# Row sums of 16384 x 1024: which rows a partition owns

## The chip, the cores and the metric

One core of one Trainium2 chip runs the kernel. The metric is device time in microseconds (us), the median of several runs. A profiled execution gives the durations of single instructions and of single DMA packets; its span runs from the first to the last instruction, and is a little shorter than the device time of the same execution.

## The reference

```python
def setup_inputs():
    batch, seq, dim = 32, 512, 1024
    return {
        "x": np.random.randn(batch, seq, dim).astype(np.float32),
        "multiplier": 0.5,
    }

def reference(x, multiplier):
    return (np.sum(x, axis=-1) * multiplier).astype(np.float32)
```

The 16384 rows of x hold 1024 floats (4 KiB) each, 67.1 MB in all; the result is one float per row, 64 KiB.

## The kernel before

The core has 128 partitions, so each of them sums 128 rows. The rows are split in three parts, in the order in which they lie in memory.

- The blocks: `own` = 112 rows for each partition, in seven blocks of 16 rows. Partition p owns the 112 rows from 112p, so a block is 16 neighbouring rows, 64 KiB in one run, for each partition.
- The tail: 15 rows for each partition (`x_last`), the 15 rows from 128 x 112 + 15p. They come in five pieces: p0 (7 rows), p1 (5), p2 (2), and the last row cut at column 608 into two pieces of its own, e0 and e1, in the tensor `end`.
- The lead: the last 128 rows of x, one for each partition (`x_lead`). It is loaded first of all, and its sums are turned by a transpose so that they are stored as four runs of 32.

All transfers are issued by SP on one queue, in this order: lead, blocks 0 to 6, p0, p1, p2, e0, e1 (line 83 in the helper `load`), the store of the blocks' results (line 167), the lead's store (171), the tail's store (195). Three buffers of 16 rows hold the blocks in turn; block b from 3 on waits until DVE has reduced block b - 3 (`freed`), and the tail's pieces wait in the same way (line 156). The lead and blocks 0 to 2 wait for nothing; `start_loads_at_entry` (line 203) moves their issues ahead of the barrier that the engines pass at the start.

DVE reduces a block in one instruction (line 134) and scales its sums (line 140). Of block 6 DVE takes eight rows, and ACT the other eight, row by row, with an activation that accumulates (`act_row`, line 90). In the tail `on_act` lists ACT's rows; DVE adds the others with `dve_sum`, which adds the two halves of a row and accumulates (line 100). The two pieces of the last row are summed one after the other, the second together with the first one's sum. The tail's store waits for both engines, and SP then waits for all three stores.

Twice the access pattern of a transfer matters. One is the source of a block, `x_rows[:, c0 : c0 + B, :]`: 128 runs of 64 KiB, 448 KiB apart. The other is the source of a tail's piece: 128 runs, 60 KiB apart.

Of the kernel before, what the change touches and what calls it, by code (L numbers as in the profile page):

```python
# [9 lines left out]
def kernel(  # L10
# [18 lines left out]
    P = nc.NUM_PARTITIONS  # L29
# [3 lines left out]
    x_flat = x.flatten_outer_dims()  # L33
    N, D = x_flat.shape
    rows = N // P
    out_flat = out.rearrange("b s -> (b s)")
    mul = float(multiplier)

    B = 16
    n_blocks = rows // B  # L40
    assert N == P * rows and rows == n_blocks * B
    own = rows - B
    tail = B - 1
    lead0 = P * (own + tail)
    x_rows = x_flat[0 : P * own, :].rearrange("(p c) d -> p c d", p=P)
    x_last = x_flat[P * own : lead0, :].rearrange("(p c) d -> p c d", p=P)
    x_lead = x_flat[lead0:N, :]
    out_rows = out_flat[0 : P * own].rearrange("(p c) -> p c", p=P)
    out_last = out_flat[P * own : lead0].rearrange("(p c) -> p c", p=P)
    out_lead = out_flat[lead0:N].rearrange("(q c) -> q c", c=32)  # L50

# [22 lines left out]
    def marks(i, engine):  # L74

        s = dve_done if engine == "dve" else act_done
        i.then_inc(s, 1)
        counts[engine] += 1
        return counts[engine]

    def load(name, dst, src, free=None):
        landed = sem(name)
        i = nc.sync.dma_start(out=dst, in_=src)  # L83
        if free is not None:
            i.wait_op(dve_done, free, "sem-ge")
        i.then_inc(landed, 16)
        return landed

    def act_row(t, r, col):
        return nc.scalar.activation(  # L90
            out=t[:, r, :],
            in_=t[:, r, :],
            func=mybir.ActivationFunctionType.Copy,
            scale=mul,
            accum_out=res[:, col : col + 1],
        )

    def dve_sum(row, dst, scale):
        mid = row.shape[-1] // 2
        return nc.vector.tensor_tensor_reduce(  # L100
            out=row[:, 0:mid],
            in0=row[:, 0:mid],
            in1=row[:, mid:],
            scale=scale,
            scalar=0.0,
            op0=ADD,
            op1=ADD,
            accum_out=dst,
        )
# [3 lines left out]
    freed = []  # L113
    lead_landed = load("lead_landed", lead, x_lead)
    for b in range(n_blocks - 1):
        c0 = b * B
        t = buf[b % bufs]
        landed = load(
            f"landed{b}",
            t,  # L120
            x_rows[:, c0 : c0 + B, :],
            freed[b - bufs] if b >= bufs else None,
        )
        h = B if b < n_blocks - 2 else B // 2
        if b == 0:
            nc.vector.wait_ge(lead_landed, 16)
            nc.vector.wait_ge(dve_done, zeroed)
            summed = marks(dve_sum(lead, lead_sq[:, 0:1], mul), "dve")
            turned = nc.vector.transpose(out=lead_tr, in_=lead_sq)  # L129
            turned.wait_op(dve_done, summed, "sem-ge")  # L130
            marks(turned, "dve")
        nc.vector.wait_ge(landed, 16)
        done = marks(
            nc.vector.reduce_sum(  # L134
                out=sums[:, c0 : c0 + h], in_=t[:, 0:h, :], axis=mybir.AxisListType.X
            ),
            "dve",
        )
        freed.append(done)
        scaled = nc.vector.tensor_single_scalar(  # L140
            out=res[:, c0 : c0 + h],
            in_=sums[:, c0 : c0 + h],
            scalar=mul,
            op=mybir.AluOpType.mult,
        )
        scaled.wait_op(dve_done, done, "sem-ge")
        early_dve = marks(scaled, "dve")
        if h < B:
            nc.scalar.wait_ge(landed, 16)
            for r in range(h, B):  # L150
                i = act_row(t, r, c0 + r)
            early_act = marks(i, "act")

    c0 = (n_blocks - 1) * B
    t = buf[(n_blocks - 1) % bufs]
    nc.sync.wait_ge(dve_done, freed[n_blocks - 1 - bufs])
    pieces = [(0, 7), (7, 12), (12, 14)]
    landed = [
        load(f"landed_p{k}", t[:, lo:hi, :], x_last[:, lo:hi, :])
        for k, (lo, hi) in enumerate(pieces)  # L160
# [11 lines left out]
    lead_stored = sem("lead_stored")  # L172
    lead_store.then_inc(lead_stored, 16)

    on_act = {4, 5, 6, 10, 11, 13}
    for k, (lo, hi) in enumerate(pieces):
        on = [r for r in range(lo, hi) if r in on_act]
        nc.scalar.wait_ge(landed[k], 16)
# [86 lines left out]
```

## Time and profile before

| What | us |
| --- | --- |
| Median of 3 runs (lowest, highest) | 160.66 (160.62, 160.67) |
| The profiled execution | 160.62 |
| its span | 159.28 |
| DVE busy (39 instructions) | 120.2 |
| ACT busy (29 instructions) | 16.3 |
| A block's reduction on DVE, 16 rows | 17.22 |
| DVE's idle time ahead of its seven reductions, all waiting for x | 30.3 |
| First reduction of a block starts | 22.81 |
| Second and third start | 42.25, 61.61 |
| Block 6: DVE and ACT start on it | 139.02 |
| The tail's store is issued | 157.80 |

DMA moved 67.18 MB in 2168 packets, 422 GB/s over the span. A reader of such a profile should ask first which resource has no gaps, and then what the start and the end add to it. "DVE" is the vector engine, "ACT" the scalar engine, "SP" the engine that issues the transfers here, "SPq" its queue of issues. A line of a timeline gives start, length, engine, source line, operation, output, input, count, and in brackets how long the engine was idle before and what ended that.

### The profile page before, as it was taken

The numbers are of one execution on the slowest core, as the hardware profiler recorded it, in microseconds if no ns is written. First come the engines' busy times: TensorE is split into PE (matmuls) and PEld (weight loads), VectorE is DVE, ScalarE is ACT, GpSimd is POOL, SyncE is SP. The second block draws the span as 40 slices with busy tenths as digits, with TensorE's granted clock in tenths as the row PEclk, the third lists the DMA queues.
The fourth block names the chain that finished last, engine by engine and source line by source line (L and its number), as shares of the span: only waits on it lengthen the run. The fifth ranks groups of instructions, "written<-read, shape, count | busy, mean of one in ns | idle before, by whom it ended". The sixth has DMA issues, their size and how long they took to land.

```text
span 159.3 us, 128 instructions
## 1 busy us (share of the span) xinstructions
DVE 120.2 (75%) x39; ACT 16.3 (10%) x29; POOL 0.2 (0%) x4
## 2 busy tenths in 40 slices
DVE  2000029999499995999869997899959999599744
ACT  2000000000000000000000000000000000099844
POOL 0000000000000000000000000000000000000000
DMA  9969989899699699699699898996996996999994
GB/s 395 510 280 527 411 379 527 379 411 527 263 527 527 263 527 527 263 527 494 296 527 428 362 527 379 411 527 280 510 527 263 527 527 263 436 403 433 442 397 144
DMA packets 2168, 67.18 MB, mean 422 GB/s; under 512 B 504, under 2 KB 632, under 8 KB 888
## 3 DMA queue, kind: packets, MB, share of 16 engines
q1 hardware_dynamic: 2168, 67.18, 98.0%
HBM read 67.11 MB, written 0.07 MB: 422 GB/s over the span
## 4 chain that ended last, share of the span: by engine, by line
DMA 75%; DVE 22%; SPq 1%; issue 0%
DMA xb<-in_x_dram 52%; DMA end<-in_x_dram 24%; DVE sums L134 22%; SPq L83 1%; DVE end L100 1%; DVE res L140 0%; DVE res L100 0%
## 5 line engine op out<-in xcount | busy, mean ns | idle before, releaser
L134 DVE TENSOR_REDUCE sums<-xb 128x16 f32<-128x16384 f32 (+1 forms) x7 | 112.0, 16001 | 30.3 <-DMA xb<-in_x_dram 30.3
L90 ACT ACTIVATE xb<-xb 128x1024 f32<-128x1024 f32 x14 | 14.6, 1046 | 138.1 <-DMA xb<-in_x_dram 138.0
L100 DVE CUSTOM_DVE_ANT_0 xb<-xb 128x512 f32<-128x512 f32 x8 | 5.1, 689 | 3.9 <-DMA xb<-in_x_dram 3.9
L90 ACT ACTIVATION_READ_ACCUMULATOR xb<-xb 128x1 f32 x14 | 2.6, 188 | 0.0
L111 DVE MEMSET end<- 128x2 f32 x1 | 0.1, 60 | 2.9 <-PEq L26 2.9
L90 ACT ACT_TABLE_LOAD x1 | 1.3, 1283 | 2.9 <-PEq L26 2.9
L140 DVE TENSOR_SCALAR res<-sums 128x16 f32<-128x16 f32 (+1 forms) x7 | 1.2, 174 | 0.2
L100 DVE CUSTOM_DVE_ANT_0 end<-end 128x304 f32<-128x304 f32 (+1 forms) x2 | 0.9, 428 | 0.1
L100 DVE CUSTOM_DVE_ANT_0 lead<-lead 128x512 f32<-128x512 f32 x1 | 0.7, 693 | 0.2 <-DMA lead<-in_x_dram 0.2
L100 DVE DVE_READ_ACCUMULATOR2_ANT res<- 128x1 f32 x9 | 0.8, 83 | 0.0
L129 DVE STREAM_TRANSPOSE lead_tr<-lead_sq 128x32 f32<-128x32 f32 x1 | 0.2, 211 | 0.0
L246 POOL MEMSET const-bfloat16-1.0<- 128x1 bf16 x1 | 0.1, 101 | 0.0
L246 POOL MEMSET const-uint8-127<- 128x1 uint8 x1 | 0.1, 101 | 0.0
L246 POOL MEMSET const-float32-0.0<- 128x1 f32 x1 | 0.1, 98 | 0.2 <-issue 0.2
L246 POOL MEMSET const-float32-1.0<- 128x1 f32 x1 | 0.1, 98 | 0.0
L112 DVE MEMSET lead_sq<- 128x32 f32 x1 | 0.1, 85 | 0.0
L100 DVE DVE_READ_ACCUMULATOR2_ANT end<- 128x1 f32 x1 | 0.1, 84 | 0.0
L100 DVE DVE_READ_ACCUMULATOR2_ANT lead_sq<- 128x1 f32 x1 | 0.1, 83 | 0.0
## 6 DMA issues: line engine op xcount, KB each, us to landing
xb<-in_x_dram SPq DMA_DIRECT2D x1, 3584.0 KB, 29.9
xb<-in_x_dram SPq DMA_DIRECT2D x1, 2560.0 KB, 35.7
xb<-in_x_dram SPq DMA_DIRECT2D x1, 1024.0 KB, 37.7
lead<-in_x_dram SPq DMA_DIRECT2D x1, 512.0 KB, 3.2
end<-in_x_dram SPq DMA_DIRECT2D x1, 304.0 KB, 37.9
end<-in_x_dram SPq DMA_DIRECT2D x1, 208.0 KB, 38.0
xb<-in_x_dram SPq DMA_DIRECT2D x7, 40.8
out_dram<-res SPq DMA_DIRECT2D x1, 56.0 KB, 9.6
```

Source lines behind the costliest of these rows:

```text
L83: i = nc.sync.dma_start(out=dst, in_=src)
L90: return nc.scalar.activation(out=t[:, r, :], in_=t[:, r, :], func=mybir.ActivationFunctionType.Copy, scale=mul, accum_out=res[:, col : co ...
L100: return nc.vector.tensor_tensor_reduce(out=row[:, 0:mid], in0=row[:, 0:mid], in1=row[:, mid:], scale=scale, scalar=0.0, op0=ADD, op1=ADD, ...
L111: marks(nc.vector.memset(end[:, at - 2 : at], 0.0), "dve")
L112: zeroed = marks(nc.vector.memset(lead_sq, 0.0), "dve")
L129: turned = nc.vector.transpose(out=lead_tr, in_=lead_sq)
L134: nc.vector.reduce_sum(out=sums[:, c0 : c0 + h], in_=t[:, 0:h, :], axis=mybir.AxisListType.X),
L140: scaled = nc.vector.tensor_single_scalar(out=res[:, c0 : c0 + h], in_=sums[:, c0 : c0 + h], scalar=mul, op=mybir.AluOpType.mult,)
L246: nc = _bacc.Bacc("TRN2", target_bir_lowering=False, num_devices=1)
```

## The change

The blocks get 111 rows for each partition instead of 112, and the tail 16 instead of 15; the lead stays. Block 0 is the one that gets shorter: 15 rows, and block b from 1 on covers the rows from 16b - 1. Partition 4g + b, with b from 0 to 3 and g from 0 to 31, owns the 111 rows from 111(32b + g): neighbouring partitions with the same g now read rows 3552 apart, and with the same b and neighbouring g rows 111 apart. The store of the blocks' results follows the same pattern. In the tail partition p owns 16 rows from 128 x 111 + 16p; the pieces are 8, 5 and 2 rows and the cut last row, and `on_act` has seven rows instead of six.

```diff
-    own = rows - B
-    tail = B - 1
+    own = rows - B - 1
+    tail = B
     lead0 = P * (own + tail)
-    x_rows = x_flat[0 : P * own, :].rearrange("(p c) d -> p c d", p=P)
+    x_rows = x_flat[0 : P * own, :].rearrange("(b g c) d -> g b c d", b=4, c=own)
     x_last = x_flat[P * own : lead0, :].rearrange("(p c) d -> p c d", p=P)
     x_lead = x_flat[lead0:N, :]
-    out_rows = out_flat[0 : P * own].rearrange("(p c) -> p c", p=P)
+    out_rows = out_flat[0 : P * own].rearrange("(b g c) -> g b c", b=4, c=own)
...
     for b in range(n_blocks - 1):
-        c0 = b * B
+        c0 = max(b * B - 1, 0)
+        n = (b + 1) * B - 1 - c0
         t = buf[b % bufs]
         landed = load(
             f"landed{b}",
-            t,
-            x_rows[:, c0 : c0 + B, :],
+            t[:, 0:n, :],
+            x_rows[:, :, c0 : c0 + n, :],
             freed[b - bufs] if b >= bufs else None,
         )
-        h = B if b < n_blocks - 2 else B // 2
+        h = n if b < n_blocks - 2 else n // 2
...
-        if h < B:
+        if h < n:
             nc.scalar.wait_ge(landed, 16)
-            for r in range(h, B):
+            for r in range(h, n):
                 i = act_row(t, r, c0 + r)
             early_act = marks(i, "act")
 
-    c0 = (n_blocks - 1) * B
+    c0 = own
...
-    pieces = [(0, 7), (7, 12), (12, 14)]
+    pieces = [(0, 8), (8, 13), (13, 15)]
...
-    on_act = {4, 5, 6, 10, 11, 13}
+    on_act = {4, 5, 6, 7, 11, 12, 14}
```

## The prediction

> **What bounds the kernel now.** I read the chain of waits first, then the busy slices, the groups by shape, the transfers' issues, the timeline of the end, and last the trace's records of single DMA packets (start, duration and size of each).
>
> The chain, in order of time (start, length, what):
>
> ```profile
> 0.90 41.33 DMA xb<-in_x_dram
> ...
> 42.25 17.23 DVE sums L134
> ...
> 59.50 40.80 DMA xb<-in_x_dram
> ...
> 100.32 17.23 DVE sums L134
> ...
> 118.91 37.93 DMA end<-in_x_dram
> ...
> 156.87 0.50 DVE end L100 x2
> 157.37 0.02 issue
> 157.39 0.38 DVE end L100
> ```
>
> The two reductions stand in it only because they free the buffer of a load that is issued long before its bytes can move. What never rests is the load:
>
> ```profile
> DMA  9969989899699699699699898996996996999994
> q1 hardware_dynamic: 2168, 67.18, 98.0%
> L134 DVE TENSOR_REDUCE sums<-xb 128x16 f32<-128x16384 f32 x6 | 103.3, 17220 | 28.3 <-DMA xb<-in_x_dram 28.3
> ```
>
> The queue's packets fill 98.0% of 16 engines' time. DVE needs 17.22 us for a block that takes 19.36 us to arrive (its reductions start at 80.97 and 100.32, 19.35 apart), so it waits 1.9 us for each. The packet records say the same: each of the seven blocks is 128 packets of 64 KiB, one per partition, 8 per engine; the median packet takes 2.418 us, and 8 x 2.418 = 19.34. In the middle of the run there is nothing left to win.
>
> What is above that floor: from the first packet (1.03 us) to the end of the last (156.92) are 155.90 us. Packets at their medians would take 8 x 0.159 (lead) + 56 x 2.418 (blocks) + 8 x (1.062 + 0.761 + 0.311 + 0.098 + 0.069) (the five pieces of the tail) = 155.09. So about 0.81 us is all that a better order of reading could give. It sits mostly at the start: the 128 packets of block 0 average 2.448 instead of 2.418, 0.24 us for an engine's eight, and the worst, the first on their engines, take 2.76 and 2.81. The other six blocks are over the median by 0.12 us together. The lead's packets are over theirs by 0.22, and the lead is not changed.
>
> **The change, part by part.** The sum is made against the profiled execution: 160.62 us, of which 159.28 is the span and 1.34 lies around it; the median of the runs is 160.66.
>
> *Rows from block 0 to the tail.* Block 0 gets 15 rows, p0 8 instead of 7, so all landings from block 0 to block 6 come earlier by one row, 19.36/16 = 1.21 us, and the tail is one row longer: the last byte comes when it did. Packet counts stay. DVE: block 0 costs 15 x 17.22/16 = 16.14, saving 1.08 in a stretch where it waits for the next block anyway. In the tail DVE keeps eight rows and ACT goes from six to seven, one more step of 1.04. ACT's four rows of p0 start at its landing, about 147.5 as now, and end near 147.5 + 4 x 1.04 + 0.19 = 151.9; p1 is started at 153.63, so 1.8 us of waiting covers it. p1 and p2 keep their split (three and two, one and one), and so does the end after them:
>
> ```profile
> 156.12 0.69 DVE L100 CUSTOM_DVE_ANT_0 xb<-xb 128x512 f32<-128x512 f32 x1 [0.57 <-DMA xb<-in_x_dram]
> ...
> 156.87 0.48 DVE L100 CUSTOM_DVE_ANT_0 end<-end 128x304 f32<-128x304 f32 x1
> ...
> 157.80 0.35 SPq L195 DMA_DIRECT2D out_dram<-res  x1
> ```
>
> Sum: 0. Without that cover the ACT step would cost 1.04.
>
> *A pattern of one more level in seven loads and the early store.* The same 128 runs, but the source now steps over 32 g and 4 b. No row of the trace has such a load. The nearest issues from both sides:
>
> ```profile
> 0.43 1.38 SPq L83 DMA_DIRECT2D xb<-in_x_dram  x3
> ...
> 148.00 0.35 SPq L167 DMA_DIRECT2D out_dram<-res  x1
> 148.39 0.62 SPq L171 DMA_DIRECT2D out_dram<-lead_tr  x1
> ```
>
> A plain 128-partition load holds SP for 1.38/3 = 0.46; the one issue that is not a plain 128-partition pattern holds it for 0.62, against 0.35 for its neighbour. So 0 to 0.27 us for each; I take 0.2. For block 0 it is covered: the lead's first packet starts 1.03 us after its issue, so block 0, issued at 0.43, could start at 1.46, with the longer issue at about 1.7; it starts at 2.45, when engines have done their lead rows. Cover 0.8 us; gone, the whole 0.2 would show. Behind it on SP are blocks 1 and 2 (needed at 22 and 41 us) and SP's arrival at the start barrier: DVE's and ACT's first work (2.94, 2.87) would come up to 0.6 later, and the first block lands past 20. Later loads wait for a free buffer and still run a block ahead: the tail's five issues start at 117.6, its data moves from 138.1. Sum: 0, bound +0.27.
>
> Should such a load use fewer of the 16 engines, nothing would hide it. The Trainium skill (DMA: Bandwidth & Descriptors, "Why a DMA increments its semaphore by 16 and not by 1") says that the number of engines is the largest up to 16 that divides the slowest dimension of both sides; that is 16 for 32 and 128, so by it nothing is lost.
>
> *The addresses.* In the blocks, neighbouring partitions read 448 KiB apart now. After, partitions with the same b and neighbouring g read 444 KiB apart, those with neighbouring b 14.2 MiB. Four partitions away, the reads are 1792 KiB apart now (7 x 256 KiB, so all are at the same place within 256 KiB), and 444 KiB after (111 x 4 KiB, so all at different places). In the tail it is the reverse: pitch 60 KiB becomes 64 KiB, four partitions 240 becomes 256 KiB. No row shows the price, so bounds: at best the blocks lose their excess, 0.24 + 0.12 = 0.36 (and 0.81 if everything above the floor went); at worst the tail gains what block 0 shows now, 0.24 at the entry of each of p0, p1 and p2, +0.72. For the blocks I take the nearest rows, the tail's packets, whose spacing now is not a multiple of 256 KiB: over their medians by 0.01 (p0) and 0.02 us (p1) for an engine's eight, against 0.24. So -0.35. For the tail I take 0, since blocks 1 to 6 are aligned now and pay only 0.02 each once the engines run out of step.
>
> [...]
>
> *Stores.* The early store (444 instead of 448 B each) moves behind the loads in the queue as now (issued at 148.00, landed 9.6 us later), and the last store carries 64 instead of 60 B. Its 128 packets take 0.010 us each, 8 per engine: 0.
>
> Sum: 160.66 - 0.35 = **160.31**.
>
> **Rivals.**
>
> *The start is not a matter of addresses (no change).* The lead's packets, which read one contiguous piece, are also over their median, by 0.22 us: then the first packets are slow whatever they read, and all else is hidden. Against it: the lead is the very first reading, block 0 is not. 160.65, 160.4 to 160.9. [...]
>
> *The tail's 64 KiB pitch (slower).* The place is p2 and the two pieces of the last row, where a packet is 8 KiB, 2432 and 1664 B and every reader is at the same place within 64 KiB. Price: from +0.24 (one more entry like block 0's) to a doubling of 8 x (0.311 + 0.098 + 0.069) = +3.8; I take +0.6, 161.3. Nothing behind the last landing can absorb it: the final sums follow it within 0.02 us. It decides as soon as these three together exceed 3.82 us by more than the 0.35 won. Against: 448 KiB pitch now costs nothing in steady running.
>
> *The jumps (much slower).* An engine that goes from one b to the next leaps 14.2 MiB. If each leap cost what the first packets of block 0 cost, 0.14 us on average over the sixteen, 56 packets would give +7.9, about 168. Against: such slow packets now occur at the start only.
>
> *The change does not alter who reads when.* If the records show block 0's packets as long as before, it did nothing to the start: this is the no-change case.
>
> The Trainium skill (DMA: Bandwidth & Descriptors, "The descriptor swizzle") gives four neighbouring partitions to one engine, so that at a time the engines would be at one b and different g; no record here names the engine.
>
> **How the numbers follow.** A difference under 0.2% (0.32 us) cannot be told from none here: faster is below 160.34, slower above 160.98. Chances: the forecast 0.44, with its own range 159.95 to 160.45; no change 0.31; the tail 0.17; the jumps 0.08. The forecast's case stays within 0.2% in about a tenth of its cases, the no-change case crosses to the fast side in as many. Faster 0.43, same 0.32, slower 0.25. The range starts at 159.9 (0.81 won, less a little) and goes to 161.4, past the tail's price; outside are the jumps, and dear tails: about 0.15.
>
> **What would show it.** Right: block 0's packets (60 KiB, 2.418 x 15/16 = 2.27 us expected) without outliers of 2.5 and more; blocks still 19.35 apart; the last landing near 156.5 instead of 156.92, and the same 0.9 us from there to the last store's issue. Wrong: outliers at block 0 as before; packets of p2 or of the last row above 0.311, 0.098 and 0.069; an issue of block 0 so long that its first packet comes after 2.45 with the engines idle; blocks more than 19.4 apart; ACT still in p0 when p1 lands.

## The result, and the profile after

The changed kernel takes 162.80 us (median of 6 runs, 162.28 to 163.47) against 160.66: a ratio of 1.0136, 95% interval 1.0124 to 1.0148, so 2.1 us slower where 0.35 us faster was forecast, and outside the range. Its profiled execution took 163.47 us with a span of 162.14. Medians here and below are over all executions; the ratios leave out six that lie over 1.5% above the fastest of their kernel (two each of e2 and e16, one each of e4 and e15), and are if anything too low there.

The page of the changed kernel: the busy tenths of the DMA engines and what they moved in 40 slices, and the queue's share.

```profile
DMA  7999998997997998998998997998998999999991
GB/s 281 318 455 440 470 446 388 453 501 340 453 501 340 469 485 356 453 485 356 453 485 356 453 501 340 453 501 372 437 485 388 437 469 396 396 412 435 395 372 51
q1 hardware_dynamic: 2168, 67.18, 96.7%
```

The same 2168 packets and 67.18 MB, with a lower share of a longer span (98.0% before). The kernel before moved, in its 40 slices:

```profile
GB/s 395 510 280 527 411 379 527 379 411 527 263 527 527 263 527 527 263 527 494 296 527 428 362 527 379 411 527 280 510 527 263 527 527 263 436 403 433 442 397 144
```

The first two slices (8 us) move 281 and 318 GB/s, before 395 and 510. Single slices go up and down between 263 and 527 in the kernel before, so this only says where to look.

The chain of waits, in order of time (start, length, what), shows whether later stretches lose as well.

```profile
0.44 0.67 SPq L83
1.11 0.04 issue
1.15 42.72 DMA xb<-in_x_dram
...
43.90 17.23 DVE sums L135
61.13 0.02 issue
61.14 40.78 DMA xb<-in_x_dram
...
101.95 17.23 DVE sums L135
...
120.53 39.15 DMA end<-in_x_dram
...
159.70 0.53 DVE end L100 x2
```

The second stretch of DMA is 40.78 long, 40.80 before. The first is 42.72 instead of 41.33, although it carries one row less. DVE's block reductions in the timeline put a number on that, first of the kernel before, then of the changed one:

```profile
22.81 17.22 DVE L134 TENSOR_REDUCE sums<-xb 128x16 f32<-128x16384 f32 x1 [18.62 <-DMA xb<-in_x_dram]
...
42.25 17.22 DVE L134 TENSOR_REDUCE sums<-xb 128x16 f32<-128x16384 f32 x1 [2.01 <-DMA xb<-in_x_dram]
```

```profile
24.54 16.15 DVE L135 TENSOR_REDUCE sums<-xb 128x15 f32<-128x15360 f32 x1 [19.55 <-DMA xb<-in_x_dram]
...
43.90 17.22 DVE L135 TENSOR_REDUCE sums<-xb 128x16 f32<-128x16384 f32 x1 [3.00 <-DMA xb<-in_x_dram]
...
63.25 17.22 DVE L135 TENSOR_REDUCE sums<-xb 128x16 f32<-128x16384 f32 x1 [1.93 <-DMA xb<-in_x_dram]
```

Block 0 lands at 24.54 instead of 22.81, and should have landed 1.21 us earlier: 1.73 + 1.21 = 2.94 us are lost by then. From there on the blocks come 19.36, 19.35, ... apart, as before. The last packet ends at 159.76 instead of 156.92, 2.83 us later, so behind block 0 no more than 0.1 us is won or lost.

The packet records show how it is lost. How many engines were moving data at each time (2.75 us to 5.5 us), with the sums over the start. "Over the usual duration" adds what block 0's packets that start before 8 us take beyond 2.418 and 2.267 us:

```
engines moving data at (us)       2.75  3.0  3.5  4.0  4.5  5.0  5.5
before                              14   16   16   16   16   16   15
changed                              7    9   10   10   12   14   16
                                              before   changed
the lead's last packet ends                     2.88      2.87
first packets of block 0 start between     2.45-2.88 2.40-5.17
longest packet of block 0                       2.81      3.65
over the usual duration, mean per engine        0.20      1.05
idle from 2.4 to 5.6 us, mean per engine        0.06      0.91
```

The lead ends as before, and then up to nine of the 16 engines have nothing to move; the last of them gets its first packet of block 0 at 5.17, which is 2.3 us after the lead's end. While they come in one by one, packets of 2.27 us take up to 3.65. Idle time and long packets together are 1.70 us more for the mean engine. The 2.83 is more than that because a block has landed only when its last engine is done.

### The profile page after: what moved, and what is told of

Read it like the earlier page. It is cut to its first block, busy times and chain, and to the rows that moved or that the text cites. A ratio compares the mean times of both kernels' runs of the same rounds, so it can differ in the third digit from the quotient of the medians.

```text
span 162.1 us, 130 instructions
## 1 busy us (share of the span) xinstructions
DVE 119.2 (74%) x39; ACT 17.3 (11%) x31; POOL 0.2 (0%) x4
## 2 busy tenths in 40 slices
DMA packets 2168, 67.18 MB, mean 414 GB/s; under 512 B 504, under 2 KB 632, under 8 KB 888
## 3 DMA queue, kind: packets, MB, share of 16 engines
q1 hardware_dynamic: 2168, 67.18, 96.7%
## 4 chain that ended last, share of the span: by engine, by line
DMA 76%; DVE 22%; SPq 1%; issue 0%
DMA xb<-in_x_dram 52%; DMA end<-in_x_dram 24%; DVE sums L135 21%; SPq L83 1%; DVE end L100 1%; DVE res L141 0%; DVE res L100 0%
## 5 line engine op out<-in xcount | busy, mean ns | idle before, releaser
L135 DVE TENSOR_REDUCE sums<-xb 128x16 f32<-128x16384 f32 (+2 forms) x7 | 110.9, 15849 | 32.2 <-DMA xb<-in_x_dram 32.2
L90 ACT ACTIVATE xb<-xb 128x1024 f32<-128x1024 f32 x15 | 15.7, 1045 | 139.1 <-DMA xb<-in_x_dram 139.1
L141 DVE TENSOR_SCALAR res<-sums 128x16 f32<-128x16 f32 (+2 forms) x7 | 1.2, 174 | 0.2
```

The source lines that it names most:

```text
L90: return nc.scalar.activation(out=t[:, r, :], in_=t[:, r, :], func=mybir.ActivationFunctionType.Copy, scale=mul, accum_out=res[:, col : co ...
L135: nc.vector.reduce_sum(out=sums[:, c0 : c0 + h], in_=t[:, 0:h, :], axis=mybir.AxisListType.X),
L141: scaled = nc.vector.tensor_single_scalar(out=res[:, c0 : c0 + h], in_=sums[:, c0 : c0 + h], scalar=mul, op=mybir.AluOpType.mult,)
```

## The experiments

Each group ran on one chip, side by side and with the kernel before, whose medians were 160.57 to 160.61. Times are medians with lowest and highest; the ratios are to the kernel before.

**First group: the rows, the form of block 0's issue, its levels, its addresses.** The builder prepares the issue of a plain load of 128 runs in advance; a switch turns this off for single loads, which makes the issue longer (0.58 us for block 0 in e2, 0.43 in the kernel before) without touching what is read.

e1, rows alone:

```diff
-    x_rows = x_flat[0 : P * own, :].rearrange("(b g c) d -> g b c d", b=4, c=own)
+    x_rows = x_flat[0 : P * own, :].rearrange("(p c) d -> p c d", p=P)
...
-    out_rows = out_flat[0 : P * own].rearrange("(b g c) -> g b c", b=4, c=own)
+    out_rows = out_flat[0 : P * own].rearrange("(p c) -> p c", p=P)
```

> The changed row counts (111 and 16) with the plain order of partitions: partition p owns 111 rows from 111p, the source of a block is one level of 128 runs again. Theory A (the loss of 2.1 us is at block 0's start and comes from the two-level load of block 0, whose issue on SP took 0.67 us instead of 0.46) and theory B (it comes from the addresses of the 4g + b order) both say 160.5 to 160.8, last landing near 156.9. The rival of the prediction, that the tail's 64 KiB pitch costs time, says 161.3 or more, with packets of p2 and the last row above 0.311, 0.098 and 0.069 us.

160.93 (160.59 to 161.36), ratio 1.0015 (1.0003 to 1.0028). In its records p2's packets are at 0.311 and those of the last row at 0.098 and 0.069, as before: the 64 KiB pitch of the tail costs nothing, and the rival is out. The rows cost 0.05 to 0.45 us, not two.

e2, the kernel before with the prepared form off for block 0; e3, the kernel before with two levels in block 0 (which so sums some other rows):

```diff
     def load(name, dst, src, free=None):
+        nc.dge_precook = name != "landed0"
         i = nc.sync.dma_start(out=dst, in_=src)
+        nc.dge_precook = True
```

```diff
+    def near(c0):
+        rows0 = x_flat[0 : 32 * 449, :].rearrange("(g k) d -> g k d", k=449)
+        rows0 = rows0[:, 0:448, :].rearrange("g (b c) d -> g b c d", b=4)
+        return rows0[:, :, c0 : c0 + B, :]
...
-            x_rows[:, c0 : c0 + B, :],
+            near(c0) if b == 0 else x_rows[:, c0 : c0 + B, :],
```

> The kernel before, with the same 128 runs and addresses in block 0; only the builder's prepared form of that one issue is switched off. Theory A1 (the longer issue as such delays the descriptors of block 0, whatever its addresses): issue of block 0 over 0.6 us, engines enter block 0 over 2 us or more instead of 0.43, time 162.3 to 163.2. Theory A2 (only the second level matters) and theory B (addresses): issue longer, start as before, 160.5 to 160.9.

> The kernel before, with a source of two levels in block 0 at nearly the old addresses: 449 rows from one group of four partitions to the next instead of 448, so that block 0 sums other rows. Theories A1 and A2: 162.3 to 163.2, with engines entering block 0 over more than 2 us. Theory B: 160.5 to 160.9.

e4, the changed kernel with block 0 in four loads:

```diff
...
+            for q in range(4):
+                i = nc.sync.dma_start(out=t[q:P:4, 0:n, :], in_=x_rows[:, q, c0 : c0 + n, :])
+                i.then_inc(landed, 16)
...
```

> The changed kernel, with block 0 in four loads of 32 partitions, one for each b: the same addresses in the same order, each load with one level. Theory B: still 162.3 or more, with first packets of block 0 at 2.7 us and above. Theory A2: back to about 160.7. Theory A1: the four issues are also long ones, so the first load comes late as in the changed kernel, 162 to 163, but the engines may be reached by a shorter list each.

e2 161.11 (160.60 to 163.06; ratio 1.0025, 1.0003 to 1.0048), e3 161.24 (160.72 to 162.62; 1.0054, 1.0025 to 1.0083), e4 161.18 (160.71 to 163.28; 1.0045, 1.0012 to 1.0078). None of the theories said this: each kernel reaches the time of the kernel before in some runs and that of the changed kernel in others. What e2 shows all the same is that the addresses are not needed: its reads are those of the kernel before, and three of ten runs took over 162, where the kernel before stayed under 161.2.

The profiled execution of e3 (161.43 us) shows a second form of the lateness. In its records all 16 engines move data from 2.75 us on, but two of block 0's first packets take 3.35 and 3.52 us instead of 2.42, and their engines end the block at 23.13 and 23.34, the other 14 by 22.61. Two late engines make nearly the whole loss.

**Second group: which of the loads matter.** The same switch for other blocks (e5: 0, 1 and 2; e6: 1 and 2; e8: 3 to 6), and e7, the changed kernel with a plain block 0:

```diff
-    x_rows = x_flat[0 : P * own, :].rearrange("(b g c) d -> g b c d", b=4, c=own)
+    x_zero = x_flat[0 : P * 15, :].rearrange("(p c) d -> p c d", p=P)
+    x_rows = x_flat[P * 15 : P * own, :].rearrange("(b g c) d -> g b c d", b=4, c=own - 15)
...
-            x_rows[:, :, c0 : c0 + n, :],
+            x_zero if b == 0 else x_rows[:, :, c0 - 15 : c0 - 15 + n, :],
...
```

> The kernel before, old addresses, with the prepared form switched off for the three loads that are issued at the start (blocks 0, 1, 2). Theory A3 (each long issue at the start adds a chance that engines get block 0's descriptors late; three of them make it the rule): 162.0 to 163.3, hardly a run under 161. Theory C (one long issue gave 161.1, the rest of the loss in the changed kernel is its addresses): about 161.1, as with block 0 alone.

> The kernel before with the prepared form switched off for blocks 1 and 2 alone. If only the load whose bytes are needed next matters: 160.5 to 160.7. If the long issues behind block 0 hold it up too (A3): above 161, with engines entering block 0 over more than 1 us.

> The changed kernel with its block 0 as a plain load of 15 neighbouring rows for each partition (from a region of its own, pitch 60 KiB); blocks 1 to 6 stay in the 4g + b order with 96 rows. Theory A (start only): 160.5 to 161.0, all of the loss gone but what the moved rows alone cost. Theory B or C (addresses): above 161.5, with long packets where block 1 begins.

> The kernel before with the prepared form switched off for blocks 3 to 6, which are issued a block or more ahead of their bytes. All theories of the start: 160.5 to 160.7. A theory by which such a load is slower on the engines at any time: above 161.

e5 162.74 (161.23 to 163.54, 4 runs; ratio 1.0115, 1.0054 to 1.0177). e6 160.55, ratio 0.9995 (0.9985 to 1.0004). e7 160.71, 1.0007 (0.9995 to 1.0020). e8 160.66, 1.0000 (0.9989 to 1.0011). So only block 0's load matters. Long issues of loads that are not needed at once cost nothing, and six blocks in the 4g + b order cost nothing: theory B, in which these reads are slow whenever they are done, is out. The chain of e6, whose blocks 1 and 2 have the long issue, starts like that of the kernel before:

```profile
0.44 0.42 SPq L84
0.86 0.04 issue
0.91 41.27 DMA xb<-in_x_dram
```

**Third group: cover, and the loads behind block 0.** e9 holds blocks 1 and 2 of the changed kernel back; e10 and e11 put F = 2 and F = 5 rows of block 0 in front of it as a plain load, from a region of their own at the start of x, and split the early store in the same way:

```diff
-            freed[b - bufs] if b >= bufs else None,
+            freed[b - bufs] if b >= bufs else summed if b else None,
```

```diff
...
+        skip = F if b == 0 else 0
+        if b == 0:
+            front_landed = load("front_landed", t[:, 0:F, :], x_zero)
         landed = load(
             f"landed{b}",
-            t[:, 0:n, :],
-            x_rows[:, :, c0 : c0 + n, :],
+            t[:, skip:n, :],
+            x_rows[:, :, c0 + skip - F : c0 + n - F, :],
...
```

> The changed kernel, but the loads of blocks 1 and 2 wait until DVE has summed the lead (about 4 us); block 0 is still the two-level load. Theory A3 (long issues right behind block 0's hold its descriptors up further): like the runs with one long issue, a median near 161.2, some runs at 160.7 and some at 163. Rival (block 0's own long issue is all that counts and its lateness is chance): as the changed kernel, 162.3 to 163.5.

> The changed kernel with the first 2 rows of block 0 as a plain load from a region of their own ahead of the two-level load of the other 13: 2.4 us more of data before the late descriptors are needed. Theory A (descriptors late by up to about 2.2 us after the lead's end): 160.6 to 161.2, the first packets of 52 KiB following the 8 KiB ones without idle engines. Theory B (the two-level reads are slow when they begin, whenever that is): 162 or more, with the long packets moved behind the 2 rows.

> The same with 5 rows in front, 6.0 us of data. Theory A: 160.5 to 160.9, no run above 161.3. Theory B: 162 or more.

e9 162.61 (162.13 to 162.90; ratio 1.0121, 1.0097 to 1.0144): theory A3 falls, the loads behind block 0 are not to blame. e10 161.38 (161.14 to 161.71), ratio 1.0052 (1.0036 to 1.0068); e11 160.70 (160.62 to 160.82), ratio 1.0007 (0.9998 to 1.0017). The loss goes with the cover: 2.0 us with none but the lead (e9), 0.8 with 2.4 us of data more, nothing that can be told with 6.0. The long issue is still there in e11, in the chain as in the timeline (four loads from 0.43 to 2.86):

```profile
0.90 0.66 SPq L86
1.56 0.04 issue
1.60 39.40 DMA xb<-in_x_dram
```

```profile
0.43 2.43 SPq L86 DMA_DIRECT2D xb<-in_x_dram  x4
...
21.66 16.15 DVE L142 TENSOR_REDUCE sums<-xb 128x15 f32<-128x15360 f32 x1 [11.11 <-DMA xb<-in_x_dram]
```

Block 0 lands at 21.66, within 0.06 of the 22.81 - 1.21 = 21.60 that the moved row should give.

**Fourth and fifth group: kernels or chips.** e12 reads block 0 of the kernel before at the changed addresses (and so sums other rows); e13 is e5 with blocks 1 and 2 held back as in e9; e14 is the changed kernel again. Then e2, e3, e4 and the changed kernel side by side as e15 to e18.

```diff
+    def far(c0):
+        rows0 = x_flat[0 : P * 111, :].rearrange("(b g c) d -> g b c d", b=4, c=111)
+        return rows0[:, :, c0 : c0 + B, :]
...
-            x_rows[:, c0 : c0 + B, :],
+            far(c0) if b == 0 else x_rows[:, c0 : c0 + B, :],
```

> The kernel before with block 0 alone read at the changed kernel's addresses (4g + b order, 111 rows from one g to the next), so that it sums other rows; all other loads as before. If the order of addresses adds to the late start: 162.1 to 163.3 in nearly every run, as in the changed kernel. If it adds nothing: 160.7 to 162.6 with a median near 161.2, as with two levels at the old addresses.

> The kernel before, old addresses and one level, prepared form off for blocks 0, 1 and 2, with blocks 1 and 2 held until DVE has summed the lead. If the long issues right behind block 0's made the difference between 161.1 (one of them) and 162.7 (three): back to a median near 161.1, with runs at 160.6. If not, so that the runs with three only fell on the late side of a spread: also about 161 to 162.7; told from the first by the same spread in both.

> The changed kernel once more, beside the two above and on their chip: 162.3 to 163.5. If its runs spread down to 160.7 as those with one long issue do, the state of the chip at the start decides and not the form of the change.

> The kernel of e2 (block 0's prepared form off, old addresses) beside the changed kernel on one chip. Theory D (the long issue of block 0 is the whole cause, and how late the engines get it differs from chip to chip): whatever the changed kernel's time is here, this one is within 0.5 us of it, about 163 if the changed kernel is at 163. Theory E (kernel e2 loses less than the changed one): near 161.1 with the changed kernel above 162.3.

> The kernel of e3 (two levels in block 0, nearly the old addresses). Theory D: within 0.5 us of the changed kernel beside it. Theory E: near 161.2 with the changed kernel above 162.3.

> The kernel of e4 (the changed kernel, block 0 in four loads of 32 partitions, one level each). Theory D: within 0.5 us of the changed kernel, unless a load of 32 partitions reaches the engines sooner. Theory E: near 161.2.

> The changed kernel beside these three on the same chip: 162.3 to 163.5 by theory E on every chip; by theory D it may also spread down to 160.7 where the other three do.

| Run | What of block 0 differs from the kernel before | us | lowest to highest | ratio, 95% interval |
| --- | --- | --- | --- | --- |
| e12 | two levels, changed addresses | 163.02 | 162.91 to 163.49 | 1.0135 to 1.0171 |
| e13 | issue form, also of blocks 1 and 2, which are held back | 163.02 | 162.88 to 163.14 | 1.0129 to 1.0163 |
| e14 | the changed kernel | 162.94 | 162.83 to 162.96 | 1.0126 to 1.0156 |
| e15 | issue form alone | 161.42 | 160.61 to 163.10 | 1.0030 to 1.0083 |
| e16 | two levels | 162.02 | 160.60 to 163.08 | 1.0039 to 1.0103 |
| e17 | four loads, changed addresses | 161.35 | 160.77 to 163.05 | 1.0038 to 1.0099 |
| e18 | the changed kernel | 161.94 | 160.89 to 162.92 | 1.0056 to 1.0117 |

On one chip all three lose 2.4 us in every run, whatever block 0's addresses and levels are. On another all four spread over 2 us, the changed kernel too, and their intervals overlap. The intervals allow theory D; by the medians e15 and e17 are 0.52 and 0.59 under e18, just over the 0.5 that was set. e13 beside e14 is the plainest pair: the reads of the kernel before, with the form of the first three block issues changed and blocks 1 and 2 held back, and the whole loss. The hold is not the cause: e12 and e14 lose as much without it on the same chip, e5 has the same three forms without it and lost 2.2 us, and the lateness is there in block 0, which is not held. The change of block 0's form alone is e2 and e15, which lose in part of their runs. The page of e13, its chain and the landing of block 0:

```profile
DMA  9979979979979969969969969969969969899980
q1 hardware_dynamic: 2168, 67.18, 96.7%
```

```profile
4.20 40.51 DMA xb<-in_x_dram
...
44.73 17.23 DVE sums L136
```

```profile
25.38 17.22 DVE L136 TENSOR_REDUCE sums<-xb 128x16 f32<-128x16384 f32 x1 [20.96 <-DMA xb<-in_x_dram]
```

Block 0 has landed at 25.38 and block 1 is reached at 44.73, in the kernel before at 22.81 and 42.25. In its records 14 engines end block 0 by 23.19 and two at 24.80 and 24.96 (before: all between 22.04 and 22.47), so two late engines are enough for the whole loss. And the other face of the same edit: the profiled execution of e15 took 160.67 us. Its chain has the long issue, 0.57, and no loss behind it:

```profile
0.43 0.57 SPq L84
1.00 0.04 issue
1.04 41.24 DMA xb<-in_x_dram
42.28 0.02 issue
42.31 17.23 DVE sums L136
```

In its records the lead ends at 3.10, block 0's first packets start between 2.65 and 3.10, and all 16 engines are busy from 2.75 on.

## Why the prediction was wrong

**The step that failed** is the pattern of one more level, "covered" by the lead at a sum of 0 with a bound of +0.27. The size of the issue was right: 0.67 us in the changed kernel against 0.46 taken for a plain one, inside the bound. What was wrong is the next thought, that data would start later by just as much as the issue lasts longer (1.46 becoming 1.7, against 2.45 when it is needed). The first engines do get block 0 in time, at 2.40, so the sign that was set, a first packet after 2.45, did not show it. Others get it up to 2.3 us after the lead's end. A cover of 0.8 us was reckoned for one engine's first packet, while 16 engines need theirs, and the bounds were taken from how long SP was held, which does not tell when the engines are served. The traces before had no row from which that could be bounded. The runs show the cause from both ends. The long form with the old reads gives the loss: in part of the runs for block 0 alone (e2, e15), in every run for three blocks on the chip of e13. More cover takes it away (e10 in part, e11), and so does a plain block 0 (e7).

**The addresses**: a gain of 0.35 was forecast, and none is there. Where block 0 starts with a plain load and the rest is in the new order (e7, e11), the time is 1.0007 times that before, with intervals that reach 0.9995 and 0.9998. The step took the 0.24 us of long packets in block 0 to come from aligned addresses. In e11 the five plain rows that now follow the lead have half of it, 20 KiB packets of 0.779 on average against 0.763 in p1 (0.13 us for an engine's eight), and the two-level part behind them has none, 1.515 on average with a median of 1.514. In other profiles block 0 is over its median by 0.12 (e15) to 0.24 us (before) at the old addresses, by 0.11 at a pitch of 444 KiB (e1) and by 0.24 at 60 KiB (e7). What is read first after the lead has long packets; the first rival, the start without regard to addresses, was right on this point.

**The tail's pitch** (the rival that was to be slower) does not decide: p2 and the last row are at 0.313, 0.098 and 0.069 us in the changed kernel. The Trainium skill (DMA: Bandwidth & Descriptors, "Latency and other measured facts") gives 207 GB/s for copies at a pitch of 512 KiB and 214 at what it calls full rate. No run here has that pitch; packets at 64 KiB take what they took at 60 (0.313 and 0.312 us for 8 KiB), and those at 444 KiB what they took at 448 (2.418 for 64 KiB).

**The jumps** do not cost: blocks come 19.36 apart.

**The moved rows** were put at 0. e1 measures 1.0015 (1.0003 to 1.0028), e7 and e11 with the same counts 1.0007 with 1 inside. So 0 to 0.45 us, small beside the rest. ACT's fourth row of p0 is covered as forecast; p0 and p1 start in the timeline of the changed kernel like this:

```profile
150.38 1.06 ACT L90 ACTIVATE xb<-xb 128x1024 f32<-128x1024 f32 x1 [1.29 <-DMA xb<-in_x_dram]
...
156.48 1.06 ACT L90 ACTIVATE xb<-xb 128x1024 f32<-128x1024 f32 x1 [1.84 <-DMA xb<-in_x_dram]
```

ACT waits 1.84 us for p1, 1.8 were forecast. **The start barrier** came 0.83 later (ACT 3.70 instead of 2.87), more than the 0.6 allowed, and hidden as forecast. **The stores** do not show: from the last sum to the end of the span it is 1.5 us in both.

The Trainium skill (DMA: Bandwidth & Descriptors, "Issuing engines are not separate DMA queues") calls the sequencer's time for initiating a transfer usually small relative to the DMA itself. That holds here for SP, 0.67 us beside 19; what the form of the issue did to the engines at the start was three to four times as much, and the runs had to show it.

Open: why engines get a load with the long issue late, and not all of them. The records show packets, not descriptors, so that these come late is inferred. Nor is it shown why packets are longer meanwhile, why some runs and some chips escape (block 0's form alone was not run on the chip of e13), or what is left of e10's 0.8 us: in its profiled execution (161.21) no engine waits for block 0, but one ends it at 21.60 and the other fifteen by 21.24.

## What to carry to other kernels

A load whose bytes are needed at once should have the plainest pattern that the kernel has, and one that steps over two levels belongs behind some 6 us of other data; here that is the difference between 162.61 (e9) and 160.70 (e11) on one chip. When cover is reckoned for a transfer, reckon it for the last of the 16 engines and not for the first packet, and do not take the time that the issuing engine is held for the time until data moves. In a stream that never rests, as this one, a lateness at the start is paid in full at the end: 2.94 us at block 0 were 2.83 us at the last packet.

## What the hardware showed that was not expected

- The form of the first three block issues, with the same reads and two of them held back, made 160.61 into 163.02 on one chip in every run (e13). Block 0's form alone did as much on two others, but only in part of the runs (160.60 to 163.10). The kernel before spread over 0.3 us beside the former and over 0.6 and 0.4 beside the latter.
- While engines are late, the packets of those that run are longer, up to 3.65 us instead of 2.27, so that fewer engines did not mean faster ones. In e3 such packets came with no engine idle.
- Engines that start apart stay apart: the last and first to begin block 1 are 2.5 us apart in the changed kernel, 0.43 before, and still 2.5 us at block 6.
